# An encoder trunk on one core: projections in units of 512 columns, another order at the front, weight splits in halves, a head's last step behind the next head's first, gates by exponentials

## The chip, the cores and the metric

The kernel runs on one core of one Trainium2 chip. The metric is the device time of one execution in microseconds (us). Such a core has a matrix engine (PE), two engines for elementwise work on 128 partitions (DVE and ACT), a general one (POOL), and an engine (SP) that here only issues transfers between HBM and the on-chip memory. Each works through its own list in order, and they meet at semaphores. PE accumulates in eight banks, used here as six single ones of 512 columns (`pa`) and one pair (`pb`).

## The reference

The reference is a trunk of two layers over 512 tokens of width 1024, in float32. Cut to what matters:

```
layer 0:  rq, rk, rv, rg, dq, dk, dv = split(x @ w_in)          # 4 heads of 128 each
          ret  = group_norm(decayed_scan(rot(rq), rot(rk), rv)) * silu(rg)
          diff = rms_norm((softmax(q1 k1) - lam * softmax(q2 k2)) @ dv) * 0.8
          mix  = concat(ret, diff) @ w_out
layer 1:  cq, ckv, krope, gq, gk, gv, gg, lr = split(x @ w_in)
          mla  = softmax(q k) @ v      # q, k, v = rms_norm(cq) @ w_uq, rms_norm(ckv) @ w_ukv
          gla  = rms_norm(gated_scan(gq, gk, gv)) * silu(gg)
          mix  = concat(mla, gla) @ w_out
both:     x = layer_norm(alpha * x + mix)
          x = layer_norm(alpha * x + moe(x))   # 32 experts of 3 matrices, 2 MB each; 2 per token
```

## The kernel before

The program has two mixers (about 0 to 300 us and 785 to 1002 us in the trace), behind each an output projection with layer norm and routing (`out_rest`), and behind that the experts (`moe`, about 338 to 785 us and 1078 to 1530 us). A projection is done with every operand split in two: `hi` is the operand rounded to a shorter format (`fp32r`), `lo` the rest. Three matmuls make one product: hi x hi, hi x lo, lo x hi. `split` (L203) does it with a cast on ACT and a subtraction on DVE.

Weights come by a stream of raw slots of 1 MB. `pump` (L137) keeps up to `ahead` raws (3) loaded; `prep_w` splits one raw into a hi and a lo slot and frees the raw; `next_w` hands the pair to a projection. The expert loads (L281, L291) come by the same slots, behind the mixer's weights, and there are 192 loads of 1 MB for each layer. A load waits until its slot is free.

Two kinds of projection exist. Token-major ones, `proj_pairs` (L371), take a unit of 256 columns (all 8 slices of the depth in one raw): for each of four tiles of 128 tokens 24 matmuls (8 slices, 3 products) with 256 columns moving, two tiles into one bank, which ACT then evicts. Feature-major ones, `proj_pair_feat` (L387), move 512 tokens.

`weave` sets the order of the mixers: it puts the steps of a projection and those of heads of attention in one list, by a table of fractions (`WINDOWS`), and that list is the order in which the instructions are written; a scheduler may still move single ones. In layer 0 a projection unit for one head stands beside the attention of the head before. A diff head has 8 steps; the last is the transposing of its normalized output, which `rms_head` (L951) forms: squares on ACT (L959), reciprocal roots on POOL (L232, L234), the scale on DVE (L962, tile `on`), then four transposes on PE (L218). A retention head ends alike (`on` from POOL L862).

At the front, `x_and_proj` (L329) transposes and splits the four tiles of x, and runs the first two units (dq/dk of head 0, dv) beside them. On POOL's queue nine small transfers (`moe_weights` L993 to L996 and `small_odd` L1470 to L1476) stand early. In layer 1 the latents come from units of 256 and 192 columns, `up()` makes q, k and v from them (384 columns a matmul), `gla_vals` projects GLA's values and gates in four units of 256, beside MLA heads 0 and 1. `ret_vg` (L818) evicts a retention gate by a Silu on ACT (L826).

Of the kernel before, what the change touches and what calls it, by code (L numbers as in the profile page):

```python
# [20 lines left out]
P = 128  # L21
D = 1024
T = 512
# [13 lines left out]
WINDOWS = ((((-0.05, 0.95), (0.05, 1.2)),  # L37
            ((0.0, 1.05), (0.2, 1.15)),
            ((0.5, 1.05), (0.2, 1.3)),
            ((-0.25, 0.95), (0.0, 1.05)),  # L40
            ((-0.1, 0.9), (0.05, 1.05)),
            ((0.15, 1.05), (-0.15, 1.25)),
            ((0.05, 1.15), (0.1, 1.0), (0.45, 1.4))),
# [4 lines left out]
            ((0.05, 1.05), (0.2, 1.0), (0.15, 1.0), (0.75, 1.75)),  # L48
            ((0.15, 1.15), (0.0, 1.1))))
# [28 lines left out]
class Kernel:  # L78
# [83 lines left out]
    def prep_w(self, early=False, parts=1, sub=None, after=None):  # L162
# [114 lines left out]

    def expect_out(self, w, order):
# [34 lines left out]
    def x_tile(self, t, x):  # L313
# [3 lines left out]
        both = self.pb() if t == 0 else None  # L317
        for a in range(2):
            ps = both[:, a * 512:(a + 1) * 512] if both else self.pa()
            pv = ps.rearrange("p (j n) -> p j n", j=4)  # L320
            for j in range(4):
                self.tr(pv[:, j, :], xv[:, 4 * a + j, :])
            self.split(self.xT[0][a][:, :, s], self.xT[1][a][:, :, s], pv)
            if not both:
                self.rel(ps)
        if both:
            self.rel(both)

    def x_and_proj(self, tiles, gens):  # L329

        for t, x in tiles:
            self.x_tile(t, x)
            if t == 0:
                self.prep_w(parts=2, sub=self.nc.gpsimd if self.l else None, after=self.after)
                self.pinned = self.l == 1
            else:
                for g in gens:
                    next(g)
        self.pinned = False
        self.run_all(*gens)  # L340
# [18 lines left out]
    def proj_tok(self, o, w, t, n):  # L359

        wh, wl = (v[:, :KJ * n].rearrange("p (j n) -> p j n", j=KJ) for v in w)
        s = slice(t * P, (t + 1) * P)
        for j in range(KJ):
            a = self.xh(j)[:, s]
            self.mm(o, a, wh[:, j, :], j == 0, False)
            self.mm(o, a, wl[:, j, :], False, False)
            self.mm(o, self.xl(j)[:, s], wh[:, j, :], False, j == KJ - 1)

    def proj_pairs(self, n, evac):

        w = self.next_w()  # L371
        for tp in range(2):
            ps = self.pa()
            pv = ps.rearrange("p (k n) -> p k n", k=2)
            for k in range(2):
                self.proj_tok(pv[:, k, 0:n], w, 2 * tp + k, n)
                if k == 0 and tp == 0:
                    self.prep_w(True)
                if k == 0:
                    yield  # L380
            evac(tp, pv)
            self.rel(ps)
            if tp == 1:
                self.free(*w)
            yield

    def proj_pair_feat(self, evac):  # L387

        w = self.next_w()
        for i in range(2):  # L390
            ps = self.pa()
            yield from self.proj_feat(ps, w, i * P, 256)
            if i == 0:
                self.prep_w(True)
# [56 lines left out]
    def out_rest(self, pool, gbuf, m):  # L451
# [87 lines left out]
        with self.tc.manual_schedule(engines={mybir.EngineType.PE, mybir.EngineType.DVE}):  # L539
# [15 lines left out]
            room()  # L555
            logits(1)
# [4 lines left out]
            turn(2)  # L561
            gather(0)
            logits(2)
# [70 lines left out]
    def run(self):  # L634
# [15 lines left out]
        self.ahead = 3  # L650
# [32 lines left out]
    def expect_even(self, w):  # L683
        def diff_qk(h):
            self.expect_cols(w, [(2048 + h * P, P), (2560 + h * P, P)])

        def diff_v(i):
            self.expect_cols(w, [(3072 + 256 * i, 256)])
# [4 lines left out]
        def ret_vg(h):  # L693
            self.expect_cols(w, [(1024 + h * P, P), (1536 + h * P, P)])

        diff_qk(0), diff_v(0)
        diff_qk(1), ret_qk(0)
# [1232 lines left out]
```

## Time and profile before

| | us |
|---|---|
| Median of 3 runs | 1560.62 (1558.66 to 1562.41) |
| The profiled execution | 1560.17, its span 1558.4 |
| PE busy | 1492.4 (96%) |
| DVE, ACT, POOL busy | 689.1 (44%), 439.8 (28%), 185.7 (12%) |
| Moved by the load queue | 444.86 MB |

The span is what the trace covers; 1.77 us of the execution lie outside it. Busy shares are over the whole span, and the stages differ: the stretches (below) tell what each is worth. In a timeline row, "x48" counts instructions of one kind in a row, and the bracket says how long the engine was idle before the first and what ended that. Matmul durations overlap, so what one costs is the distance from start to start. "PEclk" is the granted clock, in parts of 2.4 GHz.

### The profile page before, as it was taken

The numbers are of one execution on the slowest core, as the hardware profiler recorded it, in microseconds if no ns is written. First come the engines' busy times: TensorE is split into PE (matmuls) and PEld (weight loads), VectorE is DVE, ScalarE is ACT, GpSimd is POOL, SyncE is SP. The second block draws the span as 40 slices with busy tenths as digits, with TensorE's granted clock in tenths as the row PEclk, the third lists the DMA queues.
The fourth block names the chain that finished last, engine by engine and source line by source line (L and its number), as shares of the span: only waits on it lengthen the run. The fifth ranks groups of instructions, "written<-read, shape, count | busy, mean of one in ns | idle before, by whom it ended". The sixth has DMA issues, their size and how long they took to land. (4 is left out here: it accounts for less than half of the span.)

```text
span 1558.4 us, 19694 instructions
## 1 busy us (share of the span) xinstructions
PE 1492.4 (96%) x7825; PEld 889.1 (57%) x7825; DVE 689.1 (44%) x1211; ACT 439.8 (28%) x770; POOL 185.7 (12%) x278
## 2 busy tenths in 40 slices
PE   7999999989999999999999899998999999999997
PEld 6888888854444444444368787675444444444433
DVE  4555655453343343343455544364333433334334
ACT  3545523022121212112246434511212122111222
POOL 3332211210000000010022200110100000001001
PEclk9999999999999999999999899998999999999999
DMA  8311133689999999999962111287999999999993
GB/s 240 109 55 55 55 109 136 231 288 425 425 427 426 426 427 425 425 427 427 426 217 96 55 68 41 99 340 267 391 426 426 425 427 427 426 425 426 426 427 139
DMA packets 106837, 465.11 MB, mean 298 GB/s; under 512 B 12973, under 2 KB 48269, under 8 KB 57457
## 3 DMA queue, kind: packets, MB, share of 16 engines
q1 hardware_dynamic: 98848, 444.86, 70.2%
q0 software_dynamic: 6160, 12.62, 2.4%
q10 hardware_dynamic: 1728, 6.29, 1.0%
q8 instruction: 63, 1.03, 0.2%
q14 instruction: 38, 0.30, 0.1%
HBM read 462.11 MB, written 9.44 MB: 303 GB/s over the span
## 5 line engine op out<-in xcount | busy, mean ns | idle before, releaser
L213 PE MATMUL pa<-big 128*64 128x512 f32 (+3 forms) x4168 | 830.6, 460 | 7.7 <-DMA big<-in_moe_w_up_dram 3.5
L213 PEld LDWEIGHTS pa<-big 128*128 128x128 f32 (+1 forms) x4168 | 449.8, 166 | 314.2 <-issue 269.4
L213 PE MATMUL pa<-big,hs 128*64 128x512 f32 x992 | 224.8, 593 | 0.0
L1199 DVE SCALAR_TENSOR_TENSOR big<-pa,rgate,big 64x512 fp32r<-64x512 f32 x120 | 89.9, 749 | 213.7 <-ACT big L1198 213.5
L213 PE MATMUL pb<-big 128*128 128x512 f32 (+1 forms) x544 | 161.3, 435 | 10.9 <-DVE big L1053 5.7
L1154 DVE SCALAR_TENSOR_TENSOR big<-big,pb 128x1024 f32<-128x1024 f32 x112 | 134.3, 1220 | 68.9 <-PE pb L213 68.6
L213 PEld LDWEIGHTS pa<-big,hs 128*64 128x64 f32 x992 | 72.9, 137 | 140.5 <-issue 135.5
L1198 ACT ACTIVATE big<-pa,rgate 64x512 fp32r<-64x512 f32 x120 | 81.8, 682 | 219.3 <-PE pa L213 167.7
L1169 DVE TENSOR_TENSOR h<-pa,h 64x512 f32<-64x512 f32 x64 | 44.4, 694 | 218.9 <-ACT h L1168 218.9
L213 PEld LDWEIGHTS pb<-big 128*128 128x128 f32 x544 | 98.8, 191 | 57.8 <-issue 30.3
L1168 ACT ACTIVATE h<-pa 64x512 f32<-64x512 f32 x64 | 37.6, 588 | 263.9 <-PE pa L213 263.9
L203 DVE TENSOR_TENSOR big<-big 128x2048 fp32r<-128x2048 f32 (+2 forms) x38 | 77.3, 2033 | 64.3 <-ACT big L203 45.8
L203 ACT CAST big<-big 128x2048 fp32r<-128x2048 f32 (+2 forms) x39 | 64.7, 1665 | 55.5 <-PE pa L213 25.0
L1131 POOL DMA_INDIRECT big<-x1d,ridx x30 | 31.3, 1045 | 354.9 <-DVE ridx L1105 244.7
L1142 ACT COPY big<-pb 128x1024 f32<-128x1024 f32 (+1 forms) x34 | 32.5, 962 | 119.1 <-PE pb L218 119.1
L1130 POOL MEMSET big<- 128x1024 f32 x28 | 26.7, 952 | 325.8 <-PE pb L218 325.8
L218 PEld LDWEIGHTS pa<-eye,h 64*128 64x128 f32 x256 | 35.5, 209 | 37.8 <-DVE big L1199 24.3
L213 PE MATMUL pb<-big,C 128*128 128x512 f32 x192 | 54.0, 413 | 2.5 <-DVE big L1154 2.5
L218 PE MATMUL pb<-eye,big 128*128 128x128 f32 x304 | 43.6, 287 | 10.2 <-DMA big<-in_x_dram 5.5
L218 PEld LDWEIGHTS pb<-eye,big 128*128 128x128 f32 x304 | 38.9, 194 | 17.1 <-issue 11.6
L1179 DVE COPY hs<-pa 128x256 f32<-128x256 f32 x64 | 27.0, 422 | 43.8 <-PE pa L218 43.7
L213 PEld LDWEIGHTS pb<-big,C 128*128 128x128 f32 x192 | 33.3, 188 | 19.4 <-issue 9.7
(312 smaller groups left out, 1192.1 us busy)
## 6 DMA issues: line engine op xcount, KB each, us to landing
big<-in_moe_w_gate_dram SPq DMA_DIRECT2D x128, 1024.0 KB, 18.4
big<-in_moe_w_up_dram SPq DMA_DIRECT2D x128, 1024.0 KB, 19.5
big<-in_moe_w_down_dram SPq DMA_DIRECT2D x128, 1024.0 KB, 19.6
big<-in_ev_w_in_dram SPq DMA_DIRECT2D x24, 512.0 KB, 5.9
big<-in_od_w_in_dram SPq DMA_DIRECT2D x7, 1024.0 KB, 6.0
big<-in_x_dram SPq DMA_DIRECT2D x8, 512.0 KB, 4.1
big<-in_ev_w_out_dram SPq DMA_DIRECT2D x4, 1024.0 KB, 4.7
x1d<-big ACTq DMA_DIRECT2D x8, 512.0 KB, 4.8
```

The costliest lines, as they stand in the source:

```text
L203: ins = self.nc.scalar.copy(hi, src), (sub or self.nc.vector).tensor_tensor(lo, src, hi.bitcast(F32), op=OP.subtract)
L213: return self.nc.tensor.matmul(o, a, b, start=start, stop=stop, skip_group_check=True)
L218: self.nc.tensor.transpose(o, a, self.eye[s, s])
L1130: self.nc.gpsimd.memset(x, 0.0)
L1131: self.nc.gpsimd.indirect_dma_start(x, None, self.x1d[:, :], bass.IndirectOffsetOnAxis(m["idx"][:, pair:pair + 1], 0), bounds_check=T - 1, ...
L1142: self.nc.scalar.copy(xn[:, i * n:(i + 1) * n], ps[:, i * n * P:(i + 1) * n * P].rearrange("p (j n) -> p j n", j=n))
L1154: self.nc.vector.scalar_tensor_tensor(x, x, ALPHA if first else 1.0, ps, op0=OP.mult, op1=OP.add)
L1168: self.nc.scalar.activation(h, o[0:64], AF.Silu)
L1169: self.nc.vector.tensor_tensor(h, o[64:128], h, op=OP.mult)
L1179: self.nc.vector.tensor_copy(hs.rearrange("p j n -> p (j n)"), ps[:, 0:4 * CAP])
L1198: last = self.nc.scalar.activation(hi, src, AF.Copy, scale=g[a:a + 64])
L1199: self.nc.vector.scalar_tensor_tensor(yl[a:a + 64, s], src, g[a:a + 64], hi.bitcast(F32), op0=OP.mult, op1=OP.subtract)
```

## The change

- A new `proj_wide` replaces `proj_pairs`: 512 columns in one unit, for one tile of tokens at a time, its weights in two raws that hold half of the depth each. Layer 0 gets five such units (two of 256 put together), layer 1 one of 448 for the latents and two of 512 for GLA's values and gates. q/k of the retention heads stay in `proj_pair_feat`. The order of the units and loads changes with it.
- A weight is split in two halves (`parts=2`) and up to two splits ahead of use (`ahead_w`); `ahead` goes from 3 raws to 2.
- At the front all eight transposes of x tile 0 stand before its splits, tile 1's before the first projection, and the constants of layer 0 and the nine small POOL transfers behind the first unit (these behind its last rope).
- A diff or retention head's last step goes into the next head's window; its bank is given back before that step. The last two retention heads and the four GLA norms are put in an order written out by hand.
- The retention gate is x / (1 + exp(-x)), as Exp on ACT and add, reciprocal and product on DVE over 128x512, in place of Silu.
- In `out_rest` the third tile's turn and logits come before the first gather. In `up()` the copy of the roped k moves from POOL's end to its start, and splits run ahead in it.

```diff
-WINDOWS = ((((-0.05, 0.95), (0.05, 1.2)),
+WINDOWS = ((((-0.05, 0.95), (0.05, 1.05)),
+            ((0.0, 1.05), (0.2, 1.05), (0.05, 0.25)),
...
-    def prep_w(self, early=False, parts=1, sub=None, after=None):
+    def prep_w(self, early=False, parts=2, sub=None, after=None):
...
+    def expect_wide(self, w, cols):
+        n = sum(c for _, c in cols)
+        wv = w.rearrange("(p j) n -> p j n", j=KJ)
+        def load(raw, a):
+            rv = raw[:, :4 * n].rearrange("p (j n) -> p j n", j=4)
+            o = 0
+            for s, c in cols:
+                self.nc.sync.dma_start(rv[:, :, o:o + c], wv[:, 4 * a:4 * a + 4, s:s + c])
+                o += c
...
+    def proj_wide(self, n, evac):
+        w = [self.next_w()]
+        for t in range(NT):
+            ps = self.pa()
+            s = slice(t * P, (t + 1) * P)
+            for a in range(2):
+                if len(w) == a:
+                    w.append(self.next_w())
+                wh, wl = (v[:, :4 * n].rearrange("p (j n) -> p j n", j=4) for v in w[a])
+                xh, xl = self.xT[0][a], self.xT[1][a]
+                for j in range(4):
+                    self.mm(ps[:, 0:n], xh[:, j, s], wh[:, j, :], a + j == 0, False)
+                    self.mm(ps[:, 0:n], xh[:, j, s], wl[:, j, :], False, False)
+                    self.mm(ps[:, 0:n], xl[:, j, s], wh[:, j, :], False, a == 1 and j == 3)
+                if a == 0:
+                    if t:
+                        self.ahead_w()
                     yield
-            evac(tp, pv)
+            evac(t, ps[:, 0:n])
...
+            turn(2)
             logits(1)
...
-            turn(2)
+            logits(2)
             gather(0)
-            logits(2)
...
-        self.moe_weights(m)
-        self.small_odd()
+        with self.tc.issue_after(self.roped):
+            self.moe_weights(m)
+            self.small_odd()
...
+        def window(proj, head, n):
+            nonlocal rest
+            self.weave(proj, (islice(head, n - 1), n - 1), *([(rest, 1)] if rest else []))
+            rest = head
...
-            nc.scalar.activation(vg[:, 1, 2 * tp:2 * tp + 2, :], pv[:, :, 128:256], AF.Silu)
+                nc.scalar.activation(e, g, AF.Exp, scale=-1.0)
+                nc.vector.tensor_scalar(e, e, 1.0, None, op0=OP.add)
+                nc.vector.reciprocal(e, e)
+                nc.vector.tensor_tensor(g, g, e, op=OP.mult)
...
         if gate is not None:
             nc.vector.tensor_tensor(on, on, gate, op=OP.mult)
+        if done:
+            done()
         yield
...
-        self.x_and_proj(x_tiles(), [self.proj_pairs(256, latent_q), self.proj_pairs(192, latent_kv)])
+        self.x_and_proj(x_tiles(), self.proj_wide(448, latent))
...
+            nc.gpsimd.tensor_copy(k[:, :, :, 64:96], ck[:, :, None, 128:160].to_broadcast([P, NT, 4, 32]))
...
+                if t < 2:
+                    self.ahead_w()
...
-            nc.gpsimd.tensor_copy(k[:, :, :, 64:96], ck[:, :, None, 128:160].to_broadcast([P, NT, 4, 32]))
```

Three places in the lists of the engines. First PE at the end of diff head 0, before: `pt` are its probabilities, `on` its normalized output, `dqk` the next head's q and k.

```order
L213 MATMUL pa<-big 128x512 x12
L213 MATMUL pa<-dv,pt 128x128 x4
L213 MATMUL pa<-big 128x256 x32
L218 MATMUL pa<-eye,on 128x128
L213 MATMUL pa<-big 128x256 x2
L218 MATMUL pa<-eye,on 128x128
L213 MATMUL pa<-big 128x256 x2
L218 MATMUL pa<-eye,on 128x128
L213 MATMUL pa<-big 128x256
L218 MATMUL pa<-eye,on 128x128
L213 MATMUL pa<-big 128x256 x11
L218 MATMUL pa<-eye,dqk 128x128 x8
```

And the changed program at the same place:

```order
L211 MATMUL pa<-dv,pt 128x128 x4
L211 MATMUL pa<-big 128x512 x12
L211 MATMUL pa<-dv,pt 128x128 x4
L211 MATMUL pa<-big 128x512 x24
L216 MATMUL pa<-eye,dqk 128x128
L216 MATMUL pa<-eye,on 128x128
L216 MATMUL pa<-eye,dqk 128x128 x3
L216 MATMUL pa<-eye,on 128x128 x3
L216 MATMUL pa<-eye,dqk 128x128 x4
L211 MATMUL pa<-big 128x512 x12
```

Between the last matmul with `dv,pt` and the first transpose of `on` there stand 32 matmuls of 256 columns before and 24 of 512 after, with the first transposes of `dqk` now on both sides of it.

Second DVE at the same place, before: the add and rotation of a retention q/k (`rqk`, `rotb`), a weight's subtraction (`big` from `big`), and the scales of `on`.

```order
L811 TENSOR_TENSOR rqk<-pa,rcs 128x512
L812 TENSOR_TENSOR rotb<-pa,rcs 64x512
L813 TENSOR_TENSOR rotb<-pa,rcs 64x512
L203 TENSOR_TENSOR big<-big 128x2048
L962 TENSOR_SCALAR on<-pa,rmsy 128x128 x4
L210 SCALAR_TENSOR_TENSOR big<-pa,subln,big 128x512
L887 TENSOR_TENSOR dqs_877<-pa,dqs_877 64x512
```

And in the changed program, where `rotb` holds the exponentials of the gate and `rvg` the gate itself:

```order
L955 SCALAR_TENSOR_TENSOR dpe<-dpe,dzs 128x512
L201 TENSOR_TENSOR big<-big 128x1024 x3
L867 TENSOR_SCALAR rotb<-rotb 128x512
L868 RECIPROCAL rotb<-rotb 128x512
L1003 TENSOR_SCALAR on<-pa,rmsy 128x128
L869 TENSOR_TENSOR rvg<-rvg,rotb 128x512
L1003 TENSOR_SCALAR on<-pa,rmsy 128x128 x3
L929 TENSOR_TENSOR dqs_734<-pa,dqs_734 64x512
L201 TENSOR_TENSOR big<-big 128x1024
L208 SCALAR_TENSOR_TENSOR big<-pa,subln,big 128x512
```

The add and the reciprocal of a gate now stand ahead of the scales of `on`, and the rotations of `rqk` have gone elsewhere. At the end of diff head 2 the same rows stand once more, and two gates stand together before the norm of retention head 1.

Third PE between `up()` and MLA's head 0, before: `pb<-big 128x384` and `pa<-big 128x384` are `up()`, `mq` and `mk` the roped q and k, `mqk` their transposes.

```order
L218 MATMUL pa<-eye,gem 1x128
L213 MATMUL pb<-big 128x384 x4
L213 MATMUL pa<-big 128x384 x6
L213 MATMUL pb<-big 128x384 x2
L218 MATMUL pa<-eye,mk 96x128 x2
L218 MATMUL pa<-eye,mq 96x128 x2
L218 MATMUL pa<-eye,mk 96x128 x2
L218 MATMUL pa<-eye,mq 96x128 x2
L213 MATMUL pa<-big 128x256 x2
L213 MATMUL pa<-mqk_6522,mqk_6515 128x512
L213 MATMUL pa<-big 128x256 x94
```

And after:

```order
L211 MATMUL pa<-big 128x384 x2
L211 MATMUL pa<-big 128x512 x13
L211 MATMUL pb<-big 128x384 x6
L211 MATMUL pa<-big 128x512
L216 MATMUL pa<-eye,gem 1x128
L211 MATMUL pa<-big 128x512 x3
L211 MATMUL pa<-big 128x384 x6
L211 MATMUL pa<-big 128x512 x19
L216 MATMUL pa<-eye,mq 96x128 x4
L216 MATMUL pa<-eye,mk 96x128 x4
L211 MATMUL pa<-big 128x512 x12
L211 MATMUL pa<-mqk_6025,mqk_6018 128x512
```

The first matmuls of the value projection, 36 of them with 512 columns, now stand among and behind those of `up()` and ahead of the transposes of `mq`, where only two of 256 columns stood before the first product of `mqk`.

## Rows read from the trace of the kernel before

**Rows 1.** Stretches: length, busy us (instructions) of PE, PEld, DVE, ACT, POOL, clock, DMA share, GB/s.

```profile
46.00:300.00 254.00, 243.91 (x1560) 212.38 (x1561) 138.60 (x226) 104.39 (x200) 55.99 (x84) 1.00 0.30 101
345.00:785.00 440.00, 434.52 (x2084) 191.94 (x2081) 165.23 (x245) 87.23 (x126) 28.12 (x29) 1.00 1.01 423
785.00:1002.00 217.00, 208.02 (x1202) 162.67 (x1198) 104.51 (x191) 106.20 (x202) 28.55 (x52) 0.98 0.22 76
1078.00:1530.00 452.00, 446.65 (x2126) 199.85 (x2127) 167.33 (x250) 89.86 (x130) 29.36 (x31) 0.99 0.99 414
```

**Rows 2.** Waits of SP's queue: us in total, times, longest us.

```profile
SPq L291 <- PE pa L213: 338.7, 117, 19.6
```

**Rows 3.** Chain that ended last: start us, us, what.

```profile
1455.75 20.79 DMA big<-in_moe_w_up_dram
```

**Rows 4.** PE's timeline, equal matmuls: start us, us, engine line op, out<-in, count [idle <-releaser].

```profile
30.68 14.64 PE L213 MATMUL pa<-big 128*128 128x256 f32 x120
45.16 0.38 PE L218 MATMUL pa<-eye,dqk 128*128 128x128 f32 x2
...
1026.93 11.04 PE L213 MATMUL pb<-big 128*128 128x512 f32 x48
1037.81 5.61 PE L213 MATMUL pa<-big 128*128 128x512 f32 x24
```

**Rows 5.** PE's groups by shape, 0:315, then 785:1050: count, busy, mean ns, idle.

```profile
L213 PE MATMUL pa<-big 128*128 128x256 f32 x960 | 127.2, 289 | 1.5 <-ACT big L203 1.5
...
L213 PE MATMUL pa<-big 128*128 128x256 f32 x480 | 67.9, 297 | 1.7 <-DVE big L623 1.3 <-DVE gS L1857 0.3
L213 PE MATMUL pa<-big 128*128 128x192 f32 x96 | 11.5, 274 | 0.0
```

**Rows 6.** PE's timeline at the front.

```profile
10.57 0.58 PE L213 MATMUL pa<-big 128*128 128x256 f32 x1 [1.51 <-ACT big L203]
13.95 1.97 PE L218 MATMUL pa<-eye,big 128*128 128x128 f32 x8 [2.80 <-DMA big<-in_x_dram]
15.57 5.38 PE L213 MATMUL pa<-big 128*128 128x256 f32 x27
```

**Rows 7.** PE's timeline at the ends of heads of layer 0.

```profile
83.19 0.33 PE L218 MATMUL pa<-eye,on 128*128 128x128 f32 x1 [2.72 <-DVE on L962]
...
111.42 3.12 PE L213 MATMUL pa<-big 128*128 128x256 f32 x24
114.77 1.01 PE L218 MATMUL pa<-eye,on 128*128 128x128 f32 x4 [0.23 <-DVE on L962]
...
281.36 0.66 PE L218 MATMUL pa<-eye,on 128*128 128x128 f32 x4 [1.49 <-POOL on L862]
```

**Rows 8.** Single lines of DVE: ns min/median/max, first and last start, forms.

```profile
L909 DVE RECIPROCAL dzs<-dzs x32: 136/164/167, 55.7 to 182.0; 128x1 f32<-128x1 f32 x32
...
L1079 DVE RECIPROCAL y<-y x2: 178/178/179, 337.1 to 1077.0; 128x4 f32<-128x4 f32 x2
...
L811 DVE TENSOR_TENSOR rqk<-pa,rcs x8: 692/692/693, 66.1 to 233.8; 128x512 f32<-128x512 f32 x8
```

**Rows 9.** Layer 1: PE's timeline behind `up()`, and a stretch (columns as in rows 1).

```profile
879.13 0.67 PE L218 MATMUL pa<-eye,mq 128*96 128x128 f32 x2 [4.28 <-POOL mq L1496]
...
882.04 14.00 PE L213 MATMUL pa<-big 128*128 128x256 f32 x94
...
882.00:898.00 16.00, 16.00 (x109) 15.00 (x108) 3.35 (x3) 4.11 (x5) 0.00 (x0) 0.85 0.05 7
```

**Rows 10.** PE's timeline: a turn of GLA's norms, and the wait for a gather.

```profile
1014.69 0.63 PE L218 MATMUL pa<-eye,on 128*128 128x128 f32 x4 [1.21 <-DVE on L964]
...
1056.79 1.96 PE L213 MATMUL pb<-big 128*128 128x512 f32 x4 [1.64 <-DVE big L1053]
```

**Rows 11.** PE's timeline: the first expert of each layer.

```profile
337.94 10.59 PE L213 MATMUL pa<-big 128*64 128x512 f32 x48 [0.33 <-ACT big L1142]
...
1077.91 12.35 PE L213 MATMUL pa<-big 128*64 128x512 f32 x48 [0.33 <-ACT big L1142]
```

More of the change, by code (lines that the diff above doesn't have):

```diff
@@ L316, in x_tile, with x_and_proj @@
         s = slice(t * P, (t + 1) * P)
[L317 to L329, printed above, removed]
+        for js in (((0, 1),) if t == 0 else ((0,), (1,))):
+            ps = self.pb() if t == 0 else self.pa()
+            pv = ps.rearrange("p (a j n) -> p a j n", a=len(js), j=4)
+            for i, a in enumerate(js):
+                for j in range(4):
+                    self.tr(pv[:, i, j, :], xv[:, 4 * a + j, :])
+            for i, a in enumerate(js):
+                self.split(self.xT[0][a][:, :, s], self.xT[1][a][:, :, s], pv[:, i])
+            self.rel(ps)
+    def x_and_proj(self, tiles, gen):
         for t, x in tiles:
@@ L333, in x_and_proj @@
             if t == 0:
-                self.prep_w(parts=2, sub=self.nc.gpsimd if self.l else None, after=self.after)
+                self.prep_w(sub=self.nc.gpsimd if self.l else None, after=self.after)
                 self.pinned = self.l == 1
             else:
-                for g in gens:
-                    next(g)
+                next(gen), next(gen)
         self.pinned = False
-        self.run_all(*gens)
+        self.run_all(gen)
     def xh(self, j):
@@ L649, in run @@
                 self.pump()
-        self.ahead = 3
+        self.ahead = 2
         self.new_xT()
@@ L776, in mixer_even @@
         self.new_cat(0)
-        self.weave((ret_units(2), 8), (ret_head(0), 4))
-        self.weave((ret_units(3), 8), (ret_head(1), 4))
+        window((ret_qk(2), 4), ret_head(0), 4)
+        window((self.chain(wide(ret_vg(2), ret_vg(3)), ret_qk(3)), 12), ret_head(1), 4)
         self.free(*self.xbuf)
@@ L947, in diff_head, with rms_head @@
         pv(3)
-        yield from self.rms_head(pool, po, 4 + h, gsub)
-        self.rel(po)
-    def rms_head(self, pool, po, c, gain, gate=None):
+        yield from self.rms_head(pool, po, 4 + h, gsub, done=lambda: self.rel(po))
+    def rms_head(self, pool, po, c, gain, gate=None, done=None):
         nc = self.nc
@@ L1462, in expect_odd @@
         self.expect(up, n=1536)
-        for i in range(4):
-            self.expect_cols(w, [(928 + 256 * i, 256)])
+        for i in range(2):
+            self.expect_wide(w, [(928 + 512 * i, 512)])
     def small_odd(self):
@@ L1649, in mixer_odd @@
         self.residual_in(m, self.x2d)
-        self.weave((self.chain(*[self.rms_head(pool, o[:, :, h * P:(h + 1) * P], 4 + h, ggl, sg[:, :, h * P:(h + 1) * P])
-                                 for h in range(4)]), 8), (out, 2))
+        r = [self.rms_head(pool, o[:, :, h * P:(h + 1) * P], 4 + h, ggl, sg[:, :, h * P:(h + 1) * P]) for h in range(4)]
+        for g in (r[0], r[1], out, r[0], r[2], r[1], r[3], out, r[2], r[3]):
+            next(g)
+        self.run_all(*r, out)
         self.free(gvb, sgb, obuf)
```

192 lines of the change are left out of this document (93 added, 99 removed).

## The prediction

> **What bounds the kernel now.** I read the stretches first, then the waits of the load queue, then the chain that ended last, and only then PE's own timeline. The reader is to see in the stretches that there are two kinds [rows 1]. In 345:785 and 1078:1530 the DMA share is 1.01 and 0.99 at 423 and 414 GB/s: the expert stream fills them. In the mixers, 46:300 and 785:1002, the share is 0.30 and 0.22 and PE is busy for 243.91 of 254 and 208.02 of 217 us: PE sets their length. The waits say how the two kinds join: expert loads waited 338.7 us, 117 times, for matmuls to give a slot back [rows 2]. So the stream is not running at its rate ahead of the mixer's end; its slots come when the mixer and the experts' matmuls let go, and the chain at the end runs on the last loads, the first of them at 1455.75 [rows 3], which were issued when earlier experts freed slots. I conclude that a microsecond out of either mixer is a microsecond out of the total. What there is to win lies in the mixers, in three things: what a matmul costs beyond its columns, PE's idle time (10.1 us in 46:300, 9.0 in 785:1002, lengths less busy), and stretches with a granted clock under 1.
>
> **Term 1, fewer and wider matmuls: -11.3.** From start to start, 120 matmuls of 256 columns take 45.16 - 30.68 = 14.48 us, 0.1207 each; 48 of 512 take 1037.81 - 1026.93 = 10.88, 0.2267 each [rows 4]. Two narrow ones cost 0.2413, one wide 0.2267: 0.0147 less. The line through both prices gives 0.0147 as what a matmul costs beyond its columns, so two of any width put together save that. Layer 0 had 960 of 256 columns [rows 5] and gets 480 of 512; layer 1 had 480 of 256, of which 96 are the latents' and 384 GLA's, and 96 of 192 [rows 5]; it gets 96 of 448 and 192 of 512. Matmuls that go: 480 + 96 + 192 = 768, by 0.0147 = 11.3 us, all on PE's path in stretches that PE sets. Ends: 8 (evictions, now each over a whole bank, sometimes come late) to 14 (wide ones as fast as 512 / 2.4 GHz = 0.213 would save 0.028 each, 21; I don't go so far). The Trainium skill ("TensorE: Matmul & The Clock Gate", section "Back-to-back issue gap") speaks against this term: a matmul would cost N/2.4 + 2.5 ns, so that a pair put together saves 2.5 ns, and 768 of them 1.9 us. By that rule the sum below would be 9.4 us smaller. The trace doesn't agree: 0.1207 is 14 ns above 256 / 2.4, and 0.2267 is 13 ns above 512 / 2.4.
>
> **Term 2, the front: -2.** The projection's first matmul starts at 10.57 behind 1.51 us of waiting for the weight's cast, then PE waits 2.80 us for x tile 1 [rows 6], and the next 27 matmuls take 5.38 us, 0.199 each where 0.1207 is normal: 2.1 us lost among arrivals. In the new order tile 1's transposes come first, and 13 wide matmuls (2.9 us) fill the wait before the next tile; the POOL transfers no longer share the DMA engines at this time. But the x tiles and the first weight must still land, and the first unit now needs two raws, 2 MB, instead of one before it can finish a tile. I take 2 of 1.51 + 2.80 + 2.1; ends 0 and -4. The nine POOL transfers behind the first rope cost POOL's queue some time; what stands behind them is the first softmax product, which waits for a reciprocal that starts at 55.7 [rows 8], 10 us behind the first unit's end. I put it at 0, up to +2.
>
> **Term 3, layer 0's heads and gates: -2.** PE waited 2.72, 0.23 and (retention) 1.49 us at three ends of heads [rows 7]; with the others these are most of the 10.1 us. At head 1 the chain from the last product, at 111.42 + 0.24 or so, to the transposes at 114.77 took 3.4 us, nothing else in DVE's way. In the new order 24 wide matmuls, 5.4 us, stand in between at heads 0 to 2, so this wait should go: -4. Against it stand the gates. Four add chains on DVE (add, reciprocal, product over 128x512), and at heads 0 and 2 add and reciprocal stand ahead of the scales of `on`. The trace has no reciprocal of this size. One of 128x1 takes 0.164 us, one of 128x4 takes 0.178 [rows 8]: 4.7 ns a column, 164 + 511 x 4.7 = 2.6 us. Lower end: a product over the same tile, 0.69 [rows 8]. Upper end: by the shortest of the 128x1, 0.136, it is 14 ns a column, 7.3 us. I take 2.6, by the median rows. Then the chain of heads 0 and 2 is 3.4 + 0.4 + 2.6 = 6.4 us against 5.4 of cover: 1.0 lost, twice. Before the norm of retention head 1 two gates stand together: 2 x 2.6 + 1.1 = 6.3 us beside 18 matmuls (4 us) that cover the chain of another: up to 2.3, of which half is hidden by the wait that was there. Say +2 in all; ends -5 and +4 for the term at reciprocals up to 4 us. The Trainium skill ("VectorE: DVE Perf Modes", section "First, the fixed hardware budget") says that a reciprocal passes the divider with a repeat count of 8; read as eight passes it would be, by estimate, 8 x 512 / 0.96 GHz = 4.3 us, and the sum would be 4 x 1.7, some 7 us smaller. The two rows of 128x1 and 128x4 can't decide it. That ACT is spared the Silus and their table loads counts nothing: ACT is busy 104.39 of 254 us [rows 1].
>
> **Term 4, from `up()` to MLA: -4.5.** PE waits 4.28 us at 879.13 for the rope of q on POOL [rows 9]. In the new order 36 wide matmuls, 8.2 us, stand around the last steps of `up()`, and 19 (4.3 us) behind the last of these. They need GLA's value weight split by then, which `ahead_w` does in `up()`; the rope, freed of the copy of k behind it, runs beside them. They are no new work: they are taken from later. I take the 4.28 and a little of the shorter waits near it. Ends: -2 (the splits of two halves come late) and -6.5.
>
> **Term 5, the clock behind that wait: -2.5.** After it 94 matmuls of 256 columns take 14.00 us [rows 9] where 94 x 0.1207 = 11.4 would be normal; the granted clock of 882:898 is 0.85, between its two levels. If the wait goes, so does this. Ends 0 and -3.
>
> **Terms 6 and 7: -1 and -1.** A turn of GLA's norms waited 1.21 us, the gather's logits 1.64 [rows 10]; the hand-written orders put work between. I take about half of each sort over their few places. Ends +1 and -5 together.
>
> **At nothing:** splits in halves are two instructions for one, on ACT and DVE, which are busy 104.39 and 138.60 of 254 us [rows 1]; if their cover fails, a half split arrives sooner, not later. `ahead` 2 for 3: the mixers' DMA share of 0.30 and 0.22 covers it; without that cover a 1 MB load at 423 GB/s is 2.5 us for each late one.
>
> **The sum:** -11.3 - 2 - 2 - 4.5 - 2.5 - 1 - 1 = -24.3. Against the profiled execution, 1560.17 (span 1558.4 and 1.77 outside, 0.45 under the median of the runs): 1535.9, near 1536. The extremes added are far apart; taking each term's half-width (3, 3, 4.5, 2.2, 1.5, 3) as independent gives about 7.5 us to each side.
>
> **Rivals.** *A smaller gain, 1550.* Only the narrow pairs' overhead is saved, by 8 or less, with 2 at the front, because the waits come back at other places: PE's waits in the mixers are short and many, and a scheduled list that fits one spacing of matmuls doesn't fit another. For it: at head 1 the wait was just 0.23 us, so there is little to take. Against it: 4.28 us is one wait with one cause. Time: 1560 - 10 = 1550. The rule of the Trainium skill on the issue gap (its page and section stand under term 1) would lead near here too, with 1536 + 9.4 = 1545.
>
> *A larger gain, 1524.* The first expert of layer 1 takes 12.35 us for the 48 matmuls that take 10.59 in layer 0 [rows 11]: the clock falls after the idle time of `out_rest`. Should the new order there, and the better filled mixers, keep it up, and term 3 come in whole, then 1.8 + 4 + 6 more go: 1524.
>
> *No change, 1560: the expert stream sets the end.* 384 loads at 1.01 and 0.99 of the DMA engines; if a stream's start were fixed by something other than the mixer, nothing would pass through. For it: those shares. Against it: 338.7 us of its waits are for matmuls, and the share in the mixers is 0.30 and 0.22, so the start moves with PE.
>
> *Slower, 1565: the reciprocals.* At 7.3 us, the upper end, the chains of heads 0 and 2 are 11.1 us against 5.4 of cover, 5.7 lost, twice; the two gates before retention head 1 take 15.7 against 4, 11.7 lost. That is 23.1, and after three such stalls the clock costs 2.5 each, as in term 5: 7.5. Together 30.6 against a gain of 26.3 without the gates' 2: 1560.2 + 4.3 = 1564.5. It decides the sign from about 6.3 us for one reciprocal. For it: the order puts them ahead of what PE waits for. Against it: the median row is 2.6.
>
> **How the numbers follow.** Forecast 0.60, with 1527 to 1545 as its own range; smaller gain 0.18; larger gain 0.09; no change 0.06; slower 0.07. The 8-in-10 range must take in the forecast's and most of the smaller gain and half of the larger: 1523 to 1552. A measurement of this kernel tells 0.2%, about 3 us, from no change. Faster by more: 0.60 + 0.18 + 0.09 less 0.02 of the smaller gain's tail = 0.85; the same 0.08; slower 0.07.
>
> **What would show it.** Right: both mixers shorter in the changed profile, layer 0's by about 13 us and layer 1's with its routing by about 11; wide matmuls at 0.225 from start to start; no wait at `mq`; a clock of 1.00 behind it; the experts' stretches as long as before, only earlier. Reciprocals near 2.6 us, and little idle time at the ends of heads 0 to 2. Wrong: an experts' stretch that grows by what the mixer lost; reciprocals over 6 us with PE idle behind L1003 or the norm's statistics; PE waiting for a split (L201) at the start of wide units.

## The result, and the profile after

The changed kernel takes 1542.35 us (median; 1542.04 to 1542.49) against 1559.76 of the kernel before beside it: ratio 0.9886, 95% interval 0.9869 to 0.9903, 17.4 us. The forecast was 1536 with a range of 1523 to 1552. The profiled span went from 1558.4 to 1540.3.

The table cuts both spans at the same events of PE's timeline: first transposes of `dqk`, first run of output matmuls (`pb<-big`), first expert matmul, the last wait of the layer's experts for a load, and so on. Each entry is the difference of two start times.

| us | before | changed | |
|---|---|---|---|
| front, to `dqk` | 45.2 | 40.0 | -5.2 |
| heads of layer 0, to the output matmuls | 243.5 | 249.9 | **+6.3** |
| output, norm, routing | 49.3 | 46.6 | -2.7 |
| experts of layer 0 | 435.9 | 435.8 | -0.1 |
| mixer of layer 1 | 253.1 | 239.1 | **-14.0** |
| output, norm, routing | 51.0 | 48.1 | -2.9 |
| experts of layer 1 and the end | 480.5 | 481.0 | +0.5 |

So the total hides a loss: layer 1 gave more than forecast, the heads of layer 0 lost where a gain of 7 to 8 was expected. The experts' stretches kept their lengths, with the expert stream as dense as in [rows 1]. Stretches of the changed kernel (columns as there):

```profile
46.00:300.00 254.00, 238.82 (x1163) 190.35 (x1163) 152.03 (x246) 92.00 (x214) 58.96 (x88) 0.98 0.30 104
344.00:783.00 439.00, 433.66 (x2079) 191.46 (x2077) 165.21 (x245) 86.91 (x126) 28.13 (x29) 1.00 1.01 423
783.00:1000.00 217.00, 210.81 (x968) 153.47 (x965) 110.98 (x218) 112.93 (x250) 32.59 (x60) 1.00 0.28 97
1060.00:1512.00 452.00, 446.93 (x2126) 198.02 (x2123) 166.36 (x247) 89.08 (x128) 28.03 (x29) 0.99 0.99 414
```

The clock tells the two mixers apart: 1.00 to 0.98 in layer 0, 0.98 to 1.00 in layer 1. What happened at the end of diff head 0 is in PE's timeline; it answers to the first of [rows 7]:

```profile
77.61 0.27 PE L216 MATMUL pa<-eye,dqk 128*128 128x128 f32 x1
77.84 0.33 PE L216 MATMUL pa<-eye,on 128*128 128x128 f32 x1
78.01 0.49 PE L216 MATMUL pa<-eye,dqk 128*128 128x128 f32 x3
78.70 0.84 PE L216 MATMUL pa<-eye,on 128*128 128x128 f32 x3 [0.20 <-DVE on L1003]
79.39 0.60 PE L216 MATMUL pa<-eye,dqk 128*128 128x128 f32 x4
81.85 4.25 PE L211 MATMUL pa<-big 128*128 128x512 f32 x12 [1.87 <-DVE big L208]
```

The wait of 2.72 us for `on` is down to 0.20, as forecast. But the next unit waits 1.87 us for L208, which reads the transposed `on` out of a bank; then 12 matmuls take 4.05 us from start to start, 0.34 each. DVE's list at this place is full:

```profile
74.27 3.35 DVE L868 RECIPROCAL rotb<-rotb 128x512 f32<-128x512 f32 x1
77.54 0.25 DVE L1003 TENSOR_SCALAR on<-pa,rmsy 128x128 f32<-128x128 f32 x1
77.71 0.68 DVE L869 TENSOR_TENSOR rvg<-rvg,rotb 128x512 f32<-128x512 f32 x1
78.31 0.86 DVE L1003 TENSOR_SCALAR on<-pa,rmsy 128x128 f32<-128x128 f32 x3
79.20 0.68 DVE L929 TENSOR_TENSOR dqs<-pa,dqs 64x512 fp32r<-64x512 f32 x1
79.91 1.23 DVE L201 TENSOR_TENSOR big<-big 128x1024 fp32r<-128x1024 f32 x1
81.05 0.75 DVE L208 SCALAR_TENSOR_TENSOR big<-pa,subln,big 128x512 fp32r<-128x512 f32 x1
```

The reciprocal takes 3.35 us (2.6 taken, 0.69 to 7.3 as ends), and everything the next head needs of DVE queues behind it. It is not the only chain here. POOL forms the root for `on` (`rmsy`) behind the rope of the next head's `dqk`, and is done with it at 76.81:

```profile
75.76 1.05 POOL L232 TENSOR_TENSOR rmsy<-rmsv,mhalf 128x4 f32<-128x4 f32 x1
```

So of the delay of `on` itself (77.54) only some 0.7 us are the reciprocal's. The stretches of PE's wait and of what follows it:

```profile
77.00:82.00 5.00, 2.93 (x17) 1.81 (x16) 4.94 (x10) 3.02 (x7) 0.00 (x0) 1.00 0.00 0
82.00:86.00 4.00, 4.00 (x13) 3.15 (x14) 2.64 (x5) 1.74 (x3) 0.00 (x0) 0.67 0.86 247
```

DVE is busy for 4.94 of 5 us while PE waits; in the 4 us behind that the granted clock is 0.67, between its two levels of 1.2 and 2.4 GHz. At the end of head 1, where no gate stands, another wait shows:

```profile
113.57 0.69 PE L216 MATMUL pa<-eye,dqk 128*128 128x128 f32 x4 [1.60 <-POOL dqk L1538]
113.98 5.51 PE L211 MATMUL pa<-big 128*128 128x512 f32 x16
```

The q and k of the next head now come with the last matmuls of a wide unit; before, they were a unit of their own, half a window earlier. Their rope on POOL stands bare at the boundary, and the 16 matmuls behind it take 0.33 each.

At the end of head 3 the wait for `on` grew. The first row is the kernel before, the others the changed one, where POOL has a sum of the rotation of `rqk` (L852) ahead of the root:

```profile
190.30 0.33 PE L218 MATMUL pa<-eye,on 128*128 128x128 f32 x1 [0.99 <-DVE on L962]
...
193.18 0.50 PE L216 MATMUL pa<-eye,on 128*128 128x128 f32 x2 [2.55 <-DVE on L1003]
...
188.98 2.29 POOL L852 TENSOR_TENSOR rqk<-rqk,rotb 128x512 f32<-128x512 f32 x1 [7.55 <-DVE rotb L851]
```

At the front and in layer 1 the timeline answers to [rows 6] and [rows 9]:

```profile
10.51 1.97 PE L216 MATMUL pa<-eye,big 128*128 128x128 f32 x8 [2.74 <-DMA big<-in_x_dram]
12.13 4.62 PE L211 MATMUL pa<-big 128*128 128x512 f32 x13
...
26.27 13.89 PE L211 MATMUL pa<-big 128*128 128x512 f32 x60
40.00 0.38 PE L216 MATMUL pa<-eye,dqk 128*128 128x128 f32 x2
...
872.92 6.35 PE L211 MATMUL pa<-big 128*128 128x512 f32 x28
879.12 0.60 PE L216 MATMUL pa<-eye,mq 128*96 128x128 f32 x4
```

And the stretch behind `mq`:

```profile
883.00:903.00 20.00, 20.00 (x83) 14.01 (x82) 8.18 (x15) 10.95 (x20) 0.00 (x0) 1.00 0.14 45
```

From start to start 60 wide matmuls take 13.73 us, 0.229 each. No wait is left at `mq`, and the clock behind it is 1.00 where it was 0.85.

### The profile page after: what moved, and what is told of

The parts are those of the page before. It is cut to its first block, busy times and chain, and to the rows that moved or that the text cites. A ratio compares the mean times of both kernels' runs of the same rounds, so it can differ in the third digit from the quotient of the medians.

```text
span 1540.3 us, 18267 instructions
## 1 busy us (share of the span) xinstructions
PE 1477.0 (96%) x7057; PEld 843.0 (55%) x7057; DVE 707.4 (46%) x1252; ACT 432.8 (28%) x817; POOL 184.0 (12%) x278
## 5 line engine op out<-in xcount | busy, mean ns | idle before, releaser
L211 PE MATMUL pa<-big 128*64 128x512 f32 (+2 forms) x3400 | 818.4, 523 | 11.2 <-DMA big<-in_moe_w_up_dram 3.1
L211 PEld LDWEIGHTS pa<-big 128*64 128x64 f32 (+1 forms) x3400 | 400.8, 159 | 346.7 <-issue 271.6
L211 PE MATMUL pb<-big 128*128 128x512 f32 (+1 forms) x544 | 157.5, 427 | 8.8 <-DVE big L1197 4.2
L201 DVE TENSOR_TENSOR big<-big 128x1024 fp32r<-128x1024 f32 (+2 forms) x67 | 80.1, 1209 | 37.1 <-ACT big L201 31.1
L201 ACT CAST big<-big 128x1024 fp32r<-128x1024 f32 (+2 forms) x68 | 68.9, 1043 | 56.5 <-PE pa L211 38.0
L216 PE MATMUL pa<-eye,h 64*128 64x64 f32 x256 | 44.2, 293 | 0.0
```

What stands on the lines that cost most here:

```text
L201: ins = self.nc.scalar.copy(hi, src), (sub or self.nc.vector).tensor_tensor(lo, src, hi.bitcast(F32), op=OP.subtract)
L211: return self.nc.tensor.matmul(o, a, b, start=start, stop=stop, skip_group_check=True)
L216: self.nc.tensor.transpose(o, a, self.eye[s, s])
```

## The experiments

Each is the changed kernel with one edit (e5_rope and e12_best have two), timed beside the kernel before. Single runs of one kernel lie up to 10 us apart (1539.90 to 1549.86 in e6_narrow), so where medians are close the stage lengths of the profile help, and "more" and "less" are against the changed kernel's.

These lengths have a spread too. With the same code the heads of layer 0 took 249.8 to 249.9 us in three kernels and 247.0 and 247.2 in two, while PE's idle time in them was 16.7 to 16.9 us in all five. What differs is the clock. In e9_out the wait at head 0 is the same 1.87 us, but the 12 matmuls behind it take 2.86 us from start to start (4.05 in the changed kernel), at a clock of 1.00:

```profile
81.47 3.02 PE L211 MATMUL pa<-big 128*128 128x512 f32 x12 [1.87 <-DVE big L208]
...
82.00:86.00 4.00, 4.00 (x19) 3.27 (x18) 2.64 (x5) 1.74 (x3) 0.00 (x0) 1.00 0.88 256
```

So a difference in the heads under 3 us tells nothing by its length alone; PE's idle time is the steadier measure. The lists also differ beyond the edit, since a scheduler orders each program: the first transposes of `on` at head 0 come behind 24 wide matmuls in the changed kernel, 19 in e1_silu, 13 in e2_nodiv, 12 in e11_gate4.

### e1_silu

```diff
-                e = pool.tile([P, T], F32, name="rotb", bufs=2)
                 g = vg[:, 1].rearrange("p t n -> p (t n)")
-                nc.scalar.activation(e, g, AF.Exp, scale=-1.0)
-                nc.vector.tensor_scalar(e, e, 1.0, None, op0=OP.add)
-                nc.vector.reciprocal(e, e)
-                nc.vector.tensor_tensor(g, g, e, op=OP.mult)
+                nc.scalar.activation(g, g, AF.Silu)
```

> The changed kernel, with one Silu on ACT over 128x512 in place of Exp, add, reciprocal and product for each of the four gates. Theory A (the q and k of the next head now come with the last matmuls of a wide unit, so that the next head's rope, transposes and splits stand bare at the boundary): the time stays within 3 us of 1542, and PE still waits about 1.6 us for the rope of dqk at the second boundary. Theory B (the reciprocals, 3.35 us each, hold DVE up at the boundaries): some 6 to 9 us less, 1533 to 1536, with no PE wait over 1 us and a clock of 1.00 behind diff heads 0 and 2. Both: ACT gets table loads of 1.28 us back, at most 2 for each gate.

1537.86 us, ratio 0.9852 (0.9835 to 0.9869). The heads of layer 0 take 240.7 us, 9.1 less: 3.3 in PE's idle time (16.7 to 13.4) and 5.8 in busy time, which is the clock; 2.8 of these 5.8 are what comes and goes with the same code. Theory B has the heads and the clock. It does not have the total, 4.5 us less and not 6 to 9, nor the waits: 1.14 us for `on` at head 0 and 2.46 behind head 2 remain, and the wait for the rope, 1.61 us at head 1, stays as theory A had it. The total gives back less because in this run the output of layer 0 took 49.3 us (49.3 before the change, 46.6 in the changed kernel) and the first expert's 48 matmuls 12.12 us (10.59 before). PE's timeline at head 0:

```profile
78.17 0.30 PE L216 MATMUL pa<-eye,on 128*128 128x128 f32 x1 [1.14 <-DVE on L998]
...
81.07 3.02 PE L211 MATMUL pa<-big 128*128 128x512 f32 x12 [0.23 <-DVE big L208]
```

The stretch that had a clock of 0.67:

```profile
82.00:86.00 4.00, 4.00 (x20) 3.23 (x18) 2.76 (x4) 2.21 (x4) 0.00 (x0) 1.00 0.80 232
```

Of the 3.3 us of idle time 1.5 go at the end of head 3, where no gate stands. There the root is now ahead of L852 in POOL's list:

```profile
184.49 0.30 PE L216 MATMUL pa<-eye,on 128*128 128x128 f32 x1 [1.09 <-DVE on L998]
```

The same holds in e2_nodiv, e5_rope, e11_gate4 and e12_best (1.09 us there in each). So what these four and e1 win is not the reciprocal's alone.

### e2_nodiv

```diff
-                nc.vector.reciprocal(e, e)
```

> The changed kernel with the reciprocal alone left out of the gates (the gate is then x times 1 + exp(-x), so that the output is another). It is e1 without the table loads. Theory A: within 3 us of 1542. Theory B: 1533 to 1536. If e1 and this differ by more than 2 us, the table loads on ACT matter by themselves.

1537.82 us, ratio 0.9856 (0.9838 to 0.9874); heads 245.7, 4.2 less, 1.6 of it in PE's idle time (15.1). The total is that of e1 within 0.1 us, so the table loads of the Silu don't show in it. At head 0 PE still waits 2.51 us for `on`, and not for the gate: DVE stands idle until POOL gives the root, which is behind the next head's rope.

```profile
76.48 1.13 DVE L1002 TENSOR_SCALAR on<-pa,rmsy 128x128 f32<-128x128 f32 x4 [2.31 <-POOL rmsy L232]
```

So at head 0 taking the reciprocal away moves the wait (0.20 and 1.87 us in the changed kernel, 2.51 here) and doesn't shorten it.

### e3_turn

```diff
-            self.weave(proj, (islice(head, n - 1), n - 1), *([(rest, 1)] if rest else []))
-            rest = head
+            self.weave(proj, (head, n))
```

> The changed kernel with each diff or retention head's last step (the transposes of its output) back in its own window. Theory C (the moved step takes a bank of 512 columns from the next head's start and the projection waits for it, 1.87 us at the first boundary): 2 to 5 us faster than 1542. Theories A and B: the turn's cover shrinks from 24 matmuls to none behind the last product, so PE waits 2 to 5 us at each of the heads 0 to 3 and the time is 5 to 12 us longer, 1547 to 1554.

1548.12 us, ratio 0.9929 (0.9907 to 0.995); heads 252.5, 2.7 more, and PE's idle time in them 2.8 more (19.5). Theory C falls: the moved step is a gain. The total is the one that A and B gave, but not by their waits: those for `on` did not come back (0.39 us at head 1, with 12 matmuls ahead of it). The wait for the rope grew instead:

```profile
110.31 1.01 PE L216 MATMUL pa<-eye,on 128*128 128x128 f32 x4 [0.39 <-DVE on L1002]
...
115.70 1.11 PE L216 MATMUL pa<-eye,dqk 128*128 128x128 f32 x4 [3.48 <-POOL dqk L1537]
```

The head's root on POOL and the next head's rope share that queue, and now the root went first.

### e4_pair

```diff
-        wide(diff_qk(1), ret_vg(0))
-        wide(diff_qk(2), diff_v(1))
+        wide(diff_qk(1), diff_qk(2))
+        wide(diff_v(1), ret_vg(0))
```

> The changed kernel with the columns paired otherwise: q/k of heads 1 and 2 in one unit, then v of the second pair of heads with the first gate, then q/k of head 3 with the second gate. So the first boundary has the late q/k alone, the second the reciprocal alone, the third both, where in the changed kernel they are both, late q/k alone, both. Theory A: the second boundary loses its wait for the rope (1.60 us) and the clock dip behind it, some 3 us, and the first one stays as it is; 1537 to 1540 in all. Theory B: the first boundary gets clean (no 1.87 us wait, clock 1.00) and the second gets what the first had; the total within 2 us of 1542.

1546.76 us, ratio 0.9904 (0.9881 to 0.9927); heads 257.2, 7.4 more, 4.9 of it idle time. Both theories missed. At the first boundary two ropes stand on POOL ahead of the root: `on` is 4.00 us late, without any gate. At the second the rope is gone as theory A had it, but the gate now delays the next head's start. PE, then DVE:

```profile
79.79 0.90 PE L216 MATMUL pa<-eye,on 128*128 128x128 f32 x3 [4.00 <-DVE on L1003]
...
122.78 0.82 PE L211 MATMUL pb<-dkh,dqs 128*128 128x512 f32 x2 [2.44 <-ACT dkh L201]
```

```profile
115.79 3.35 DVE L868 RECIPROCAL rotb<-rotb 128x512 f32<-128x512 f32 x1
...
120.72 0.68 DVE L929 TENSOR_TENSOR dqs<-pa,dqs 64x512 fp32r<-64x512 f32 x1
```

A boundary is thus a chain over POOL, ACT and DVE, and whichever is given more work becomes the wait.

### e5_rope

```diff
-            self.rope_tok(dpool, ..., t // 2)
+            self.rope_tok(dpool, ..., t // 2, self.nc.vector if t == 3 else None)
```

(and the Silu of e1)

> The changed kernel with the Silu gates of the first experiment, and the rope of the last two token tiles of each diff head's q/k on DVE instead of POOL (six operations of 128x64; DVE is free there once the reciprocals are gone). Theory A2 (behind a wide unit the rope on POOL, 2.5 us of it in front of the head's root on the same queue, is what PE waits for at the boundaries: 1.49 us at the front, 1.61 at the second, and 1.1 for the scaled outputs): these waits go, layer 0 gets 3 to 5 us shorter than with the Silu alone, 1533 to 1535 in all. Theory B2 (the rest of the boundary's chain on DVE and ACT, splits and casts, sets the start of the next head, so that six more operations on DVE only move the wait): within 2 us of the 1537.9 with the Silu alone.

1537.88 us, ratio 0.986 (0.9835 to 0.9884); heads 239.0 against 240.7. The waits for the rope go (1.49, 1.61), and 0.59 and 1.15 us for the casts of `dkh` come at head 1. Theory A2's mechanism is seen. Its size, 1.8 us of the 3 to 5, is under the spread of the heads; 1.2 of it is idle time (13.4 to 12.2). The total can't tell it.

### e6_narrow

```diff
-        for i in range(2):
-            self.expect_wide(w, [(928 + 512 * i, 512)])
+        for i in range(4):
+            self.expect_wide(w, [(928 + 256 * i, 256)])
```

(and `gla_vals` in two units of 256)

> The changed kernel with the value and gate projections of layer 1 in four units of 256 columns instead of two of 512, all else (halves of depth, splits, order) alike: 384 matmuls for 192. By the price of rows (0.0147 us more for each pair) the layer-1 mixer gets 2.8 us longer; by a fixed cost of 2.5 ns a matmul 0.5 us. From start to start a matmul of 256 columns takes 0.121 us by the first, 0.109 by the second.

1541.22 us, ratio 0.9901 (0.9867 to 0.9936): the total can't tell. The mixer of layer 1 takes 240.9 us, 1.8 more (238.9 to 239.4 in the kernels with the changed one's code there), and 24 narrow matmuls take 2.95 us from start to start, 0.123 each:

```profile
907.10 3.12 PE L211 MATMUL pa<-big 128*128 128x256 f32 x24
910.05 1.02 PE L211 MATMUL pa<-mqk,mqk 96*128 96x512 f32 x2
```

The price by rows (0.121, 2.8 us) is nearer than 0.109 and 0.5; some of the narrow ones' cost hides in waits, since PE is busy 2.5 us longer and idle 0.7 us less.

### e7_noahead

```diff
-                if t < 2:
-                    self.ahead_w()
```

> The changed kernel without the early splits inside the step that makes q, k and v of layer 1. If the 17 us won in layer 1 come for the most part from the matmuls put between the last of these projections and the transposes of mq, that wait of some 4 us and the low clock behind it (2.5 us) come back: 1548 to 1550. Rival: the copy of the roped k at the start, and wide units, are enough: within 2 us of 1542.

1542.86 us, ratio 0.9891 (0.9868 to 0.9914). The mixer of layer 1 takes 239.5, 0.5 more. The rival holds, though which of its two parts does it was not tried: one half is split in the step before, the second while it is used, and 37 wide matmuls still stand ahead of `mq`:

```profile
870.79 8.53 PE L211 MATMUL pa<-big 128*128 128x512 f32 x37
879.16 0.60 PE L216 MATMUL pa<-eye,mq 128*96 128x128 f32 x4
```

### e8_pooldma

```diff
+        self.moe_weights(m)
+        self.small_odd()
         self.x_and_proj(...)
...
-        with self.tc.issue_after(self.roped):
-            self.moe_weights(m)
-            self.small_odd()
```

> The changed kernel with the nine small transfers on POOL's queue at the start of the program, as before the change. The first transposes of dqk come at 40.0 us in the changed kernel, 45.16 before it. Theory: the early transfers share the DMA engines with x and the first weights, and these land later: dqk 1.5 to 3 us later, the time 1544 to 1545. Rival: the order of x tiles and the wide first unit give the front's gain: dqk at 40 to 40.5, the time within 1 us of 1542.

1544.49 us, ratio 0.99 (0.9881 to 0.992). `dqk` comes at 42.8, 2.8 us later, and all that follows moves with it. The theory holds; x tile 1 is what came late, its transposes at 13.57 (10.0 to 11.1 in the changed kernel and the other runs):

```profile
13.57 1.97 PE L216 MATMUL pa<-eye,big 128*128 128x128 f32 x8 [6.39 <-DMA big<-in_x_dram]
```

### e9_out

```diff
-            turn(2)
             logits(1)
...
+            turn(2)
             gather(0)
+            logits(2)
```

(with `turn(2)`, `logits(2)` taken from their new places)

> The changed kernel with out_rest's old order (turn and logits of the third tile behind the first gather's placing). If the order gives what the stretch from the first 48 output matmuls to the first expert got shorter by (2.7 us in layer 0, 2.9 in layer 1), both come back and the time is 1546 to 1548, with 1.6 us of waiting at the gather in each layer. Rival: most of it was the clock, which fell there before (the 8 gather matmuls took 5.40 us against 3.70) and would now stay up whatever the order: within 2 us of 1542.

1544.38 us, ratio 0.991 (0.9879 to 0.9942). The stretch from output to experts takes 49.3 in layer 0, 2.7 more, and 49.2 in layer 1, 1.0 more. By length that tells nothing: with the new order the same stretches took 46.5 to 49.3 and 47.5 to 51.9 in the other kernels. The total lies between the two expectations. But both waits are back:

```profile
316.43 1.95 PE L211 MATMUL pb<-big 128*128 128x512 f32 x4 [1.58 <-DVE big L1096]
...
324.46 5.40 PE L211 MATMUL pb<-big 128*128 128x512 f32 x8 [0.68 <-DVE big L1096]
...
1043.25 1.95 PE L211 MATMUL pb<-big 128*128 128x512 f32 x4 [1.65 <-DVE big L1096]
```

PE's idle time in the two stretches is 4.8 us each, against 3.9 each in the changed kernel, so the order is worth about 1 us a layer. The 8 gather matmuls take 5.40 us in layer 0 (3.70 in the changed kernel), which is the clock, and not the order's doing: in layer 1 they took 3.70 here with the wait there, and in e1 they took 6.31 in layer 0 with the new order.

### e10_parts

```diff
-    def prep_w(self, early=False, parts=2, ...
+    def prep_w(self, early=False, parts=1, ...
```

> The changed kernel with each weight split in one piece instead of two halves (the first one apart, which was in halves before too). Theory: the halves let the first matmuls of a unit start after half a split, and this together with the split ahead is what fills the wait at mq in layer 1; with whole splits layer 1's mixer gets 3 to 6 us longer and layer 0's heads 2 to 4, 1547 to 1551. Rival: with two splits ahead the size of a piece doesn't matter: within 2 us of 1542.

1546.65 us, ratio 0.9924 (0.99 to 0.9948), runs from 1540 to 1549, the profiled one the fastest. Heads of layer 0 252.6, 2.8 more, as forecast, with 3.0 more of idle time (19.7); mixer of layer 1 1.1 more, less than the 3 to 6 expected. PE's wait for `on` at head 2 (0.58 in the changed kernel) shows it:

```profile
161.55 1.12 PE L216 MATMUL pa<-eye,on 128*128 128x128 f32 x4 [5.02 <-DVE on L1003]
```

### e11_gate4

```diff
-            if t == NT - 1:
-                e = pool.tile([P, T], F32, name="rotb", bufs=2)
-                g = vg[:, 1].rearrange("p t n -> p (t n)")
+            e = pool.tile([P, P], F32, name="rotb", bufs=2)
+            g = vg[:, 1, t, :]
```

(the four operations as they were, on these)

> The changed kernel with the gate formed token tile by token tile, as each is evicted: four times Exp, add, reciprocal and product over 128x128 in place of once over 128x512. The work on DVE stays (and four fixed costs are added, about 1 us a gate), but only the last quarter, some 1.4 us, stands at the boundary instead of 4.6. Theory B (the block at the boundary costs the 9.1 us between this gate and the Silu in layer 0's heads): 6 to 9 us of them go, with the clock at 1.00 there; 1534 to 1537. Rival (DVE's total work costs it): within 2 us of 1542.

1537.15 us, ratio 0.9862 (0.9831 to 0.9893); heads 242.8, 7.1 less, with more work on DVE in all (156.6 us busy over 40:290 against 153.4). So the amount of DVE's work is not what costs. But of the 7.1 only 2.7 are idle time, 1.5 of these at head 3 as in e1; the rest is the clock. At head 0 PE still waits 2.10 us, with DVE idle for 1.90 of it until POOL gives the root:

```profile
75.86 0.30 PE L216 MATMUL pa<-eye,on 128*128 128x128 f32 x1 [2.10 <-DVE on L1001]
```

Its reciprocals (min, median, max in ns), beside 3343/3353/3354 for the four of the changed kernel:

```profile
L866 DVE RECIPROCAL rotb<-rotb x16: 893/944/954, 47.9 to 229.0; 128x128 f32<-128x128 f32 x16
```

### e12_best

The edits of e11_gate4 and e5_rope together, without the Silu.

> The changed kernel with the gate tile by tile and the last rope of each diff head's q/k on DVE, the two edits that made layer 0's heads shorter without Silu. If they add (7.1 us and 1.8 us, each against its own kernel), the stretch from the first transposes of dqk to the output projection takes 241 us, and the time is 1534 to 1536; if DVE is now the engine that the boundary waits for, 243 us or more and 1537 or above.

1534.16 us (five runs), ratio 0.9828 (0.9809 to 0.9847): the fastest of all, some 8 us under the changed kernel. The heads of layer 0 take 238.2, 11.7 less; the two gains alone were 7.1 and 1.8, so they add, and what is over lies within the spread. PE's idle time in them is 9.4 us, for the first time less than before the change (10.5). With the rope off POOL and the gate in quarters both chains of head 0 are short. PE's waits at head 0 and behind head 2 are down to

```profile
76.22 0.30 PE L216 MATMUL pa<-eye,on 128*128 128x128 f32 x1 [0.31 <-DVE on L1001]
...
152.52 3.02 PE L211 MATMUL pa<-big 128*128 128x512 f32 x12 [0.93 <-DVE rotb L851]
```

## Why the prediction was right in sum and wrong in one step

**The sum** was in part luck. Layer 0's mixer was to get about 13 us shorter and got 1.1 longer (-5.2 and +6.3); layer 1's with its routing was to get about 11 shorter and got 16.9. The two misses have opposite signs, and so the total came 6 us from the forecast.

**That mixer time passes through** held: the experts' stretches changed by -0.1 and +0.5 us, and in e4 and e8 the front and the heads moved by +6.9 and +2.8 us and the span by +6.3 and +3.0. The rival "no change" is out.

**Term 1 (-11.3)** held as a price: 0.229 for a wide matmul (0.227 taken), 0.123 for a narrow one, 1.8 of 2.8 us on layer 1 by e6. Of its pairs 372 lie in layer 0's heads, worth 5.5 us, and the gain is there under the loss of term 3: in e1, where the clock stays at 1.00 through the heads as it did before the change, PE is busy in them for 227.4 us against 233.0.

**Term 2 (-2)** was low. Front, -5.2, less 108 pairs (1.6) is -3.6, near the end of the stated range; some 2.8 of it are the nine POOL transfers (e8), which the prediction named without a size.

**Term 3 (-2) failed.** The heads of layer 0 became 6.3 us longer where terms 1 and 3 wanted 7.5 less. The term itself measured +11.8, outside -5 to +4: 6.1 us of idle time (10.5 to 16.7) and 5.7 of low clock. In the two profiles with the shorter heads it is +9.1. Three things were wrong.

- The cover was right where it stood and was not everywhere. At heads 0 to 2 the waits for `on` went from 2.72, 0.23 and 1.17 us to 0.20, none and 0.58, and the moved step is worth 2.8 us of idle time (e3). At head 3 the wait grew from 0.99 to 2.55, behind L852 on POOL.
- The reciprocal was set against one consumer, `on`. In the trace it holds up all that the next head needs of DVE, and the bank of `on` with it. The stalls can bring a low clock, which the prediction charged only to the rival. Term 3 priced the gates at 2 us; e1, e2 and e11, which relieve DVE at the boundary, have totals 4.5, 4.5 and 5.2 us lower. How much of that is the reciprocal and how much the order of the lists, which changed with it, is not shown. The two gates before retention head 1, priced at up to 2.3, left no wait at all (its transposes at 254.85).
- A wide unit delivers the next head's q and k with its last matmul, which no part of the prediction saw. Their rope on POOL comes ahead of the root for `on`. At head 0 that chain is as long as the reciprocal's: with the reciprocal gone or in quarters PE waits 2.51 and 2.10 us there (e2, e11), and only with the rope moved as well 0.31 (e12).

The slower rival had the stall and the low clock, at 7.3 us a reciprocal. The smaller gain's mechanism, waits that come back at other places, is what happened in layer 0.

**Terms 4 and 5 (-7)** were right, and term 5 low. The mixer of layer 1 lost 14.0 us: 4.2 by its 288 pairs, 5.2 by PE's idle time (13.7 to 8.5; the wait at `mq` alone was 4.28), and the other 4.6 by the clock, which was 0.88 over 860:882 and 0.85 over 882:898 and is 1.00 in both now. The cause named was wrong in part: the early split in `up()` gives 0.5 (e7), halves 1.1 (e10). What remains, units that can begin with half the depth and the copy of the roped k at the start, was not tried alone.

**Terms 6 and 7 (-1 and -1)** held in idle time: PE's waits in GLA's norms went from 2.8 to 1.6 us, its idle time at the output fell by 0.9 and 1.3 us, and e9 brings about 1 us a layer of this back. The rest of the -5.6 at the output is the clock, which differs as much between kernels with the same order there. The larger gain's condition did not come: the first expert of layer 1 still takes 12.29 us for its 48 matmuls (12.35 before).

## What to carry to other kernels

Where heads follow each other, look at the boundary as several chains over all engines. Price an added operation by everything queued behind it there, and look for the chain that is as long: shortening one of two moved the wait, shortening both took it away. The same gate cut in four and spread over the window took 5 us off the total. A wider unit saves the fixed part of each matmul, but it hands over its first result as late as its last: ask who needs which columns first. Cut the spans at equal events before trusting a total: here +6 and -14 stood behind -17. Then look at a stage in several kernels that share its code, before a difference of 3 us is given a cause.

## What the runs showed of the hardware that was not expected

- A reciprocal on DVE costs 6.3 ns a column: (3353 - 944) ns / 384 columns, with some 0.14 us fixed. The two small shapes of [rows 8] gave 4.7. Eight passes at 0.96 GHz, the estimate that was made from the Trainium skill ("VectorE: DVE Perf Modes", section "First, the fixed hardware budget"), would be 8.3 ns; the measurement decides, at the time of six.
- The same wait of PE need not bring the same clock. In five profiles with the same code for layer 0's heads PE waits 1.86 or 1.87 us at the end of head 0, after shorter waits. In the changed kernel the granted clock over the next 4 us is 0.67, between the two levels of 1.2 and 2.4 GHz, with PE busy throughout, and it falls in e7 and e8 too; their 12 wide matmuls take 0.34 to 0.36 us each. In e6 and e9 it stays at 1.00, and they take 0.24. The heads are 2.6 to 2.9 us longer in the first three, at equal idle time. What decides it is not shown here.
